# Feed-forward elementwise steps of a two-layer trunk: two-operand work on VectorE alone instead of VectorE and GpSimd

## The chip, the cores and the metric

The kernel runs on one core of one Trainium2 chip. The metric is device time in microseconds (us), the median of the runs. TensorE multiplies matrices, VectorE (DVE in the profile), ScalarE (ACT) and GpSimd (POOL) do elementwise work, SyncE (SP) issues the DMAs.

## The reference

A trunk of two layers over 1024 latent tokens and 256 context tokens, 1024 wide. Layer 0 has neighbourhood attention, layer 1 sliding-window attention; each layer then has a gated feed-forward network with a convolution over positions (width 2816, three taps). Everything is float32. What the change touches is the feed-forward network:

```python
def conv_ffn(h, w_up, conv_w, conv_b, w_down):
    t = h.shape[1]
    u = h @ w_up
    u_p = jnp.pad(u, ((0, 0), (CONV_W // 2, CONV_W // 2), (0, 0)))
    u = sum(u_p[:, tap:tap + t] * conv_w[tap] for tap in range(CONV_W)) + conv_b
    a, g = jnp.split(u, 2, axis=-1)
    return (a * jax.nn.silu(g)) @ w_down
...
        x = x + gt1 * (o @ w_out)
...
        h = modulate(rmsnorm(x, g_ffn[i]), sh2, sc2)
        x = x + gt2 * conv_ffn(h, ffn_w_up[i], ffn_conv_w[i], ffn_conv_b[i], ffn_w_down[i])
```

Layer 0 does the same for the context tokens.

## The kernel before, in words

**Precision.** Each operand of a matmul is split in two rounded parts, hi (a ScalarE copy) and lo (the operand less hi, a two-operand subtraction). A product is three matmuls: hi by hi, lo by hi, hi by lo. So each weight block that comes from memory (`wraw`, 128 x 1024) costs one ScalarE step (`whi`) and one subtraction (`wlo`).

**The up-projection.** It goes over 22 tiles of 128 channels (`plan_up`, lines 1680 to 1841), in a form with seven block products instead of eight (`PROD`, line 1675). Before the products, four two-operand steps on 128 x 512 (`s_op`, lines 1716 to 1725, tile `s`) make sums and differences of the two weight blocks; four `wlo` follow (three of 1024 columns, one of 512). TensorE writes the PSUM banks `ua`, `uc` and `ud`; a ScalarE copy or a VectorE add (`out_p`, line 1754) empties each into `c`, which frees the bank for TensorE. Then, for each half of the gate: ScalarE's centre tap makes `u` from `c`, two VectorE steps of three operands add the other taps (`u<-c,cv,u`, line 1797), SiLU goes over the gate half (ScalarE `u<-u`), and one product of 128 x 1024 multiplies the halves (`u<-u` as a two-operand step, line 1804). One or three subtractions (`ghit`, `glot`, lines 1824 to 1839) form the blocks for the down-projection, which go to `g_dram`. In layer 0, 40 small products for layer 1's modulation stand between these matmuls (line 1847).

**The down-projection** (`plan_pair`, line 1893) goes over 11 pairs of tiles in five passes; it loads `graw` from `g_dram` and `wraw`, splits both (`ghi`, `glo`, `whi`, `wlo`), forms weight differences in `s3`, and multiplies into `dn`. The results are added to `xn`.

**Around them** stand the output projection of the attention (`plan_oproj`; `oacc`, weights `woraw` split in `Oproj.weights`), the norms' sums of squares (`plan_sums`: ScalarE squares `sq`, two-operand adds into `nsum`), then `mp` and `bc`, two small groups of matmuls that average the sums and spread the result. In layer 0, `plan_next` prepares layer 1's norms, the rope tables `rc` and `rs` (always on GpSimd, line 2056) and the first weight slabs.

**What sets the order.** A planner, `Sched` (line 89), simulates the engines once while the program is built. Each step names its engine and a duration; a step with two engines goes to the one on which it would end first (`pick_engine`, line 156). A step takes its turn by a key among those that are ready; buffers come from rings (`caps`). The instructions are then written in the order found, and each engine runs its own in that order. The attentions of the two layers and the two feed-forward networks are four separate plans. Before the change most two-operand steps of the feed-forward plans name both engines:

```python
        LO = {512: (("dve", "pool"), (t_dve(512), t_pool(512))), 1024: (("dve", "pool"), (t_dve(1024), t_pool(1024)))}
        ADD = (("pool", "dve"), (t_pool(512), t_dve(512)))
...
            eng = LO[1024] if ft == FT - 1 else ("pool", t_pool(1024))
```

`LO` serves `wlo`, `glo` and the block differences, `ADD` the `s` steps and the last adds into `xn`; the product of the halves goes to GpSimd but for one tile of each layer. The planner counts 0.065 + n/960 us for VectorE and 0.15 + n/480 us for GpSimd.

Of the kernel before, what the change touches and what calls it, by code (L numbers as in the profile page):

```python
# [14 lines left out]
ALU = mybir.AluOpType  # L15
# [5 lines left out]
T = 1024  # L21
# [7 lines left out]
FT = FF // P  # L29
# [59 lines left out]
class Sched:  # L89
# [6 lines left out]
                                       pool=(0.15, 0.08, 0.06, 0.1), dma=(0.0, 0.0, 0.0, 0.0)).items()  # L96
# [145 lines left out]
def trunk_kernel(ctx, tc, xperm, xseq, cc, wmod, bmod, gnorm, na_wqkv, na_gq, na_gk, na_bias, na_wo,  # L242
# [3 lines left out]
    act, dve, pool, pe, dma = [InOrder(tc, e) for e in (nc.scalar, nc.vector, nc.gpsimd, nc.tensor, nc.sync)]  # L246
# [177 lines left out]
    ENG = dict(pe=pe, act=act, dve=dve, pool=pool, dma=dma)  # L424
# [4 lines left out]
    def t_dve(n):  # L429
        return 0.065 + n / 960.0  # L430
# [7 lines left out]
    def t_pool(n):  # L438
        return 0.15 + n / 480.0
# [374 lines left out]
    class Oproj:  # L814
# [3 lines left out]
        def __init__(self, sc, l, c, n, psa, gate, c_gate, w_gate):  # L818
            self.sc, self.l, self.c, self.n, self.psa, self.gate, self.c_gate, self.w_gate = sc, l, c, n, psa, gate, c_gate, w_gate
            self.ot, self.acc, self.w, self.raw = {}, {}, {}, {}  # L820

        def o_tiles(self, c):
            if c not in self.ot:
# [18 lines left out]
        def weights(self, i, src, key, uses, after=()):  # L842
            sc = self.sc

            def load(e):
                self.raw[i] = rpool.tile([P, 1024], F32, tag="raw", name="woraw")
                dma.dma_start(self.raw[i], src)

            def hi(e):
                self.w[i] = w_pair()  # L850
                act.activation(self.w[i][0], self.raw[i], AF.Copy)

            def lo(e):
                ENG[e].tensor_tensor(out=self.w[i][1], in0=self.raw[i], in1=self.w[i][0].bitcast(F32), op=ALU.subtract)
            r = ("woraw", i)
            sc.op("dma", 1.8, load, reads=self.w_gate + list(after), writes=[r], key=key, acq=[("raw", r, 2)])
            sc.op("act", t_act(1024), hi, reads=[r], writes=[("woh", i)], key=key, acq=[("w", ("wo", i), uses)], rel=[r])
            sc.op(("pool", "dve"), (2.28, 1.13), lo, reads=[r, ("woh", i)], writes=[("wol", i)], key=key, rel=[r])

        def project(self, dt, key, parts, evac):  # L860

# [17 lines left out]
    slabs = Slabs(na_wqkv, WL0)  # L879
# [100 lines left out]
    sc = Sched(dict(CAPS, klt=1))  # L980
# [282 lines left out]
    def ffn(l, opj, xt1, todo):  # L1263
# [8 lines left out]
        sc = Sched(dict(b=8, raw=3, w=WBUFS, x=8, sr=SRB, g=GB, g2=GB, sq=2), {"b", "raw", "w", "x", "sr", "g", "g2", "sq"})  # L1272
# [18 lines left out]
        def sub(e, out, a, b):  # L1291
            ENG[e].tensor_tensor(out=out, in0=a, in1=b, op=ALU.subtract)

        LO = {512: (("dve", "pool"), (t_dve(512), t_pool(512))), 1024: (("dve", "pool"), (t_dve(1024), t_pool(1024)))}
        ADD = (("pool", "dve"), (t_pool(512), t_dve(512)))

        X = [None] * 3
        n_todo = len(todo)
# [5 lines left out]
        def plan_sums(nm, n, x, xtok, key, rel=lambda k: (), make=None, ring="g", first=0):  # L1304

            J = {}
            I = (f"nm{nm}",)
            for k in [(first + k) % KT for k in range(KT)]:
                def sq(e, k=k):
                    if k == first:  # L1310
                        J["t"] = make(e) if make else sr_tile("nsum")
                        J[k] = J["t"]
                    elif ring == "g":
                        J[k] = gp.tile([P, 512], F32, tag="ghi", name="sq", bufs=GB)
                    else:
                        J[k] = D_["p"].tile([P, 512], F32, tag="sq", name="sq", bufs=2)
                    act.activation(J[k][:, :n], x(k), AF.Square)
                sc.op("act", t_act(n), sq, reads=[xtok(k)] + ([("dp",)] if ring == "sq" else []),
                      writes=[I + ("sq", k)] if k != first else [I + ("sums",)], key=key(k),
                      acq=[(ring, I + ("sq", k), 1)] if k != first else [("raw", I, 1) if make else ("sr", I, 9)], rel=rel(k))  # L1320
                if k != first:
                    def add(e, k=k):
                        ENG[e].tensor_tensor(out=J["t"][:, :n], in0=J["t"][:, :n], in1=J[k][:, :n], op=ALU.add)
                    sc.op(("pool", "dve"), (t_pool(n), t_dve(n)), add, reads=[I + ("sq", k), I + ("sums",)],
                          writes=[I + ("sums",)], key=key(k), rel=[I + ("sq", k)])
            return J

# [273 lines left out]
        def t34_(i):  # L1601
            if not t34:
# [3 lines left out]
              writes=[("dsh",)], key=-50)  # L1606
        rx = lambda c, k, n=1: [("xt", c, k // 2)] * n if c or not last else []
        kb = 46.0 * n_todo
        for k in range(KT):
            key = 46.0 * (1 if not last else 0) + k  # L1610
# [17 lines left out]
        for step in range(3):  # L1628
            for j in range(4):
                key = kb + (30.0 * j + 4 * step if not last else 2.0 * j + 8 * step)  # L1630
                sh = shift[:, j + 4:j + 5]
                if step == 0:
                    plan_t(1, 512, Nm[1], j, xap(1), xtok(1), scale, key)
                    sc.op("dve", t_dve(512), lambda e, j=j: dve.tensor_tensor(
                        out=X[0][:, j, :], in0=X[1][:, j, :], in1=X[0][:, j, :], op=ALU.subtract), reads=[("x", 1, j)],
                        writes=[("x", 0, j)], key=key)
                    parts(0, j, lambda j=j: t12h()[:, 2 * j, :], lambda j=j: t12l(j)[:, 0, :], ("t1", j), key, ())
                elif step == 1:
                    plan_t(1, 512, Nm[1], j + 4, xap(1), xtok(1), scale, key)
                    sc.op("dve", tst, stt(0, j, 1, j + 4, sh, 0, j), reads=[("x", 1, j + 4)], writes=[("x", 0, j)], key=key,  # L1640
                          rel=rx(1, j + 4))
                    parts(0, j, lambda j=j: t12h()[:, 2 * j + 1, :], lambda j=j: t12l(j)[:, 1, :], ("t2", j), key, rx(0, j))
                else:
                    sc.op("dve", tst, stt(1, j, 1, j + 4, dsh[:, j:j + 1], 1, j), reads=[("x", 1, j + 4), ("dsh",)],
                          writes=[("x", 1, j)], key=key, rel=rx(1, j + 4))
                    parts(1, j, lambda j=j: t34_(0)[:, j, :512], lambda j=j: t34_(1)[:, j, :512], ("t3", j), key, rx(1, j), hcs)
                    sc.op("dve", tst, stt(0, j + 4, 0, j + 4, sh, 0, j), reads=[("x", 0, j)], writes=[("x", 0, j + 4)], key=key,
                          rel=rx(0, j))
# [5 lines left out]
        for j in range(4):  # L1654
            key = kb + (30.0 * j + 12 if not last else 2.0 * j + 24)
            k = j + 4
            sc.op("act", t_act(512), lambda e, j=j, k=k: act.activation(b2h()[:, j, :], X[1][:, k, :], AF.Identity,
                                                                        bias=shift[:, k:k + 1]),
                  reads=[("x", 1, k), ("hcfree",)], writes=[("b2", j, "h")], key=key, rel=rx(1, k))
            sc.op("dve", tst, lambda e, j=j, k=k: dve.scalar_tensor_tensor(  # L1660
                out=b2l()[:, j, :], in0=X[1][:, k, :], scalar=shift[:, k:k + 1], in1=b2h()[:, j, :].bitcast(F32), op0=ALU.add,
# [18 lines left out]
        def plan_up(pos):  # L1680
            ft = FTS[pos]
            key = KU + 19.2 * pos
# [3 lines left out]
            T = lambda *a: ("up", ft) + a  # L1686
# [23 lines left out]
            def s_op(e, t, c, make, a, b, op):  # L1710
                if make:
# [5 lines left out]
                  reads=[rg],  # L1717
                  writes=[T("s", 1)], key=pk, acq=[("sr", T("s14"), 2)], rel=[rg])
# [4 lines left out]
                  reads=[ra, rg, T("s", 2)], writes=[T("s", 3)], key=pk, rel=[ra, rg])  # L1723
# [60 lines left out]
            for part in (1, 0):  # L1784
# [15 lines left out]
                    sc.op("dve", t_dve(1024) + 0.06, conv_, reads=cs, writes=[v], key=key - 10, rel=[ct])  # L1800
                if part:
                    sc.op("act", t_act(1024), lambda e: act.activation(V[1], V[1], AF.Silu), writes=[v], key=key - 10)
            eng = LO[1024] if ft == FT - 1 else ("pool", t_pool(1024))
            sc.op(*eng, lambda e: ENG[e].tensor_tensor(out=V[0], in0=V[0], in1=V[1], op=ALU.mult), reads=[T("v", 1)],
                  writes=[T("v", 0)], key=key - 10, rel=[T("v", 1)])


# [228 lines left out]
    def plan_next(sc, KS, xn, bank, x_tile, plan_sums, plan_bc, plan_t, plan_hilo, u_done):  # L2036
# [68 lines left out]
        for i in range(AHEAD):  # L2105
            key = KS[5] - 4
            sc.op("dma", 1.4, lambda e, i=i: slabs.load(i), reads=[("dw", 4, FT // 2 - 4, "r")], writes=[("slr", i)], key=key,
                  acq=[("raw", ("slr", i), 2)])
            sc.op("act", t_act(768), lambda e, i=i: slabs.hi(i), reads=[("slr", i), ("dw", 4, FT // 2 - 1, "wl", 0)],
                  writes=[("slh", i)], key=key, acq=[("w", ("slw", i), 1)], rel=[("slr", i)])  # L2110
            sc.op(("dve", "pool"), (0.87, 1.75), lambda e, i=i: slabs.lo(i, e), reads=[("slr", i), ("slh", i)],
                  writes=[("sll", i)], key=key, rel=[("slr", i)])

    slabs = Slabs(sw_wqkv, WL1)
# [356 lines left out]
```

## Time and profile before

| | us |
|---|---|
| median of 3 runs (2942.97 to 2950.92) | 2948.2 |
| the profiled execution | 2948.73 |
| its span, first to last instruction | 2947.0 |
| TensorE busy | 2829.2 |
| VectorE busy | 2406.0 |
| ScalarE busy | 1725.0 |
| GpSimd busy | 786.1 |

The span holds, in order: layer 0's attention to about 747 us, its output projection, the context's feed-forward network (860 to 1036), layer 0's up-projection (to 1498) and down-projection (to 1710), layer 1's attention (to 2190), its output projection and norms (to 2290), its up-projection (to 2726) and down-projection. An instruction's line is nearly always 79, that of the helper which records it, so steps are told apart by tile names: `out<-in`. "Idle before, releaser" says how long an engine stood still before a step and whose signal ended that. TensorE's busy time is modelled and its matmuls overlap; how often and for whom it waits tells more than its share.

### The profile page before, as it was taken

Reading aid. Unit: us, or ns where it says so; the run is one execution under the profiler, and the core shown is the slowest. Engines: PE = TensorE matmul, PEld = TensorE weight load, DVE = VectorE, ACT = ScalarE, POOL = GpSimd, SP = SyncE. Lnnn points to the kernel's source line nnn. Section 1 sums busy time; section 2 is a strip of 40 time slices with the busy share of each in tenths; the row PEclk is TensorE's granted clock in tenths of the full one; section 3 lists DMA queues with packets and bytes.
Section 4 is the critical chain, followed back from the end, with each engine's and each line's share of the span. In section 5 each row is a group of like instructions: output and inputs, shape, how many; then the busy total and the mean of one; then the engine's idle time right before and its main releaser. Section 6 shows DMA issues by size and latency. Waiting matters only on the chain. (4 is left out here: it accounts for less than half of the span.)

```text
span 2947.0 us, 46322 instructions
## 1 busy us (share of the span) xinstructions
PE 2829.2 (96%) x16344; PEld 2456.0 (83%) x16344; DVE 2406.0 (82%) x5112; ACT 1725.0 (59%) x3392; POOL 786.1 (27%) x860
## 2 busy tenths in 40 slices
PE   6999999999999999999989999999999999999999
PEld 4999999998789977777778888899877687777787
DVE  7888888889688788788786889999987887888757
ACT  4777777778456544444444558887863544444443
POOL 2222222223100034223340134544511123433200
PEclk9999999999999999999999999999999999999999
DMA  6222222214645544444465540000244332233655
GB/s 239 62 86 79 85 59 80 86 58 148 229 150 186 181 151 139 150 145 144 156 228 177 187 137 30 24 21 14 74 134 135 102 104 100 90 100 129 242 158 186
DMA packets 138842, 367.21 MB, mean 125 GB/s; under 512 B 20849, under 2 KB 30577, under 8 KB 137201
## 3 DMA queue, kind: packets, MB, share of 16 engines
q1 hardware_dynamic: 138608, 364.24, 37.3%
q8 instruction: 129, 2.11, 0.3%
q14 instruction: 105, 0.85, 0.1%
HBM read 297.21 MB, written 66.98 MB: 124 GB/s over the span
## 5 line engine op out<-in xcount | busy, mean ns | idle before, releaser
L79 DVE TENSOR_TENSOR wlo<-wraw,whi 128x512 fp32r<-128x512 f32 (+1 forms) x245 | 300.3, 1226 | 40.0 <-ACT whi L79 38.3
L79 ACT ACTIVATE whi<-wraw 128x512 fp32r<-128x512 f32 (+1 forms) x264 | 212.2, 804 | 164.5 <-PE ud L79 44.4
L79 ACT ACTIVATE whi<-s 128x1024 fp32r<-128x1024 f32 (+1 forms) x120 | 113.2, 944 | 256.0 <-PE uc L79 222.6
L79 DVE TENSOR_TENSOR ptlo<-pt,pthi 128x512 fp32r<-128x512 f32 (+2 forms) x384 | 223.1, 596 | 44.0 <-ACT pthi L79 41.8
L79 DVE SCALAR_TENSOR_TENSOR u<-c,cv,u 128x1023 f32<-128x1023 f32 x176 | 250.4, 1438 | 8.9 <-ACT u L79 7.3
L79 PE MATMUL dn<-glo,whi 128*128 128x512 f32 x616 | 242.7, 394 | 4.7 <-DVE glo L79 4.7
L79 PE MATMUL dn<-ghi,whi 128*128 128x512 f32 x616 | 242.7, 394 | 4.2 <-ACT ghi L79 4.2
L79 ACT ACTIVATE S<-S,m 128x640 f32<-128x640 f32 (+3 forms) x288 | 221.0, 768 | 43.2 <-DVE m L79 32.5
L79 PE MATMUL dn<-ghi,wlo 128*128 128x512 f32 x616 | 242.0, 393 | 0.0
L79 ACT ACTIVATE pthi<-pt 128x512 fp32r<-128x512 f32 (+2 forms) x384 | 194.3, 522 | 62.1 <-PE pt L79 53.0
L79 PE MATMUL pt<-idr,S 128*128 128x128 f32 x1280 | 198.3, 276 | 5.8 <-DVE S L79 2.7
L79 ACT ACTIVATE ghi<-graw 128x512 fp32r<-128x512 f32 x154 | 95.8, 629 | 170.8 <-PE dn L79 96.2
L79 PE MATMUL mm<-whi,h0hi 128*128 128x384 f32 x512 | 181.2, 354 | 1.6 <-ACT qraw L79 1.6
L79 POOL TENSOR_TENSOR u<-u 128x1024 f32<-128x1024 f32 x42 | 108.0, 2572 | 270.9 <-DMA wraw<-in_w_up_dram 104.4
L79 DVE TENSOR_TENSOR glo<-graw,ghi 128x512 fp32r<-128x512 f32 x145 | 104.2, 723 | 84.6 <-ACT ghi L79 84.0
L79 PE MATMUL mm<-wlo,h0hi 128*128 128x384 f32 x512 | 172.3, 336 | 0.0
L79 PEld LDWEIGHTS pt<-idr,S 128*128 128x128 f32 x1280 | 150.1, 141 | 19.1 <-DVE ptlo L79 3.5
L79 POOL TENSOR_TENSOR qy<-qv,mhalf 128x4 f32<-128x4 f32 (+2 forms) x120 | 125.0, 1043 | 140.7 <-DVE qv L79 131.7
L79 PE MATMUL pv<-ptlo,v 128*128 128x256 f32 (+1 forms) x688 | 154.0, 298 | 4.8 <-DVE ptlo L79 4.4
L79 PE MATMUL pv<-pthi,v 128*128 128x256 f32 (+1 forms) x688 | 149.6, 290 | 8.1 <-ACT pthi L79 3.7
L79 DVE TENSOR_TENSOR wlo<-s,whi 128x1024 fp32r<-128x1024 f32 (+1 forms) x114 | 133.8, 1174 | 28.7 <-ACT whi L79 27.7
L79 PE MATMUL ua<-t12hi,whi 128*128 128x512 f32 x352 | 141.5, 402 | 11.9 <-ACT c L79 8.2
(338 smaller groups left out, 9207.2 us busy)
## 6 DMA issues: line engine op xcount, KB each, us to landing
wraw<-in_w_up_dram SPq DMA_DIRECT2D x132, 512.0 KB, 3.4
wm<-in_wmod_dram SPq DMA_DIRECT2D x80, 512.0 KB, 4.2
wraw<-in_w_down_dram SPq DMA_DIRECT2D x44, 512.0 KB, 3.5
graw<-g_dram SPq DMA_DIRECT2D x44, 512.0 KB, 4.4
wraw<-in_w_down_dram SPq DMA_DIRECT2D x88, 256.0 KB, 3.1
graw<-g_dram SPq DMA_DIRECT2D x66, 256.0 KB, 2.8
slab<-in_na_wqkv_dram SPq DMA_DIRECT2D x32, 384.0 KB, 3.2
woraw<-in_na_wo_dram SPq DMA_DIRECT2D x24, 512.0 KB, 4.6
```

The costliest lines, as they stand in the source:

```text
L79: r = f(*a, **k)
```

## The change

Inside the feed-forward plans all two-operand elementwise steps name VectorE alone. `LO` and `ADD` become single-engine entries, with 0.03 us more per step in the planner's count; the product of the halves, the norms' adds, the output projection's weights inside these plans and the first slabs of layer 1 follow. GpSimd keeps its steps of the attention plans, the small power steps of the norms and the rope tables.

```diff
@@ Oproj
+            self.w_engs = ("pool", "dve"), (2.28, 1.13)
...
-            sc.op(("pool", "dve"), (2.28, 1.13), lo, reads=[r, ("woh", i)], writes=[("wol", i)], key=key, rel=[r])
+            sc.op(*self.w_engs, lo, reads=[r, ("woh", i)], writes=[("wol", i)], key=key, rel=[r])
@@ ffn
-        LO = {512: (("dve", "pool"), (t_dve(512), t_pool(512))), 1024: (("dve", "pool"), (t_dve(1024), t_pool(1024)))}
-        ADD = (("pool", "dve"), (t_pool(512), t_dve(512)))
+        LO = {n: ("dve", t_dve(n) + 0.03) for n in (512, 1024)}
+        ADD = LO[512]
+        opj.w_engs = LO[1024]
@@ plan_sums
-                    sc.op(("pool", "dve"), (t_pool(n), t_dve(n)), add, reads=[I + ("sq", k), I + ("sums",)],
+                    sc.op("dve", t_dve(n), add, reads=[I + ("sq", k), I + ("sums",)],
@@ plan_up
-            eng = LO[1024] if ft == FT - 1 else ("pool", t_pool(1024))
-            sc.op(*eng, lambda e: ENG[e].tensor_tensor(out=V[0], in0=V[0], in1=V[1], op=ALU.mult), reads=[T("v", 1)],
+            sc.op(*LO[1024], lambda e: ENG[e].tensor_tensor(out=V[0], in0=V[0], in1=V[1], op=ALU.mult), reads=[T("v", 1)],
@@ plan_next
-            sc.op(("dve", "pool"), (0.87, 1.75), lambda e, i=i: slabs.lo(i, e), reads=[("slr", i), ("slh", i)],
+            sc.op("dve", 0.87, lambda e, i=i: slabs.lo(i, e), reads=[("slr", i), ("slh", i)],
```

By the built programs 196 instructions leave GpSimd for VectorE: 42 products of 128 x 1024, 78 `s` steps, 23 `wlo` of 512 columns and 5 of 1024, 18 `ghit`, 9 `glo`, 9 `nsum`, and 12 others.

The planner finds new orders. First place: VectorE in layer 1's up-projection, one tile from the first `u` (taps of the gate half) to the add that empties `ud` (`c<-c,ud`). Before:

```order
L79 SCALAR_TENSOR_TENSOR u<-c_28507,cv,u 128x1023
L79 TENSOR_TENSOR wlo<-wraw,whi 128x512
L79 SCALAR_TENSOR_TENSOR u<-c_28507,cv,u 128x1023
L79 SCALAR_TENSOR_TENSOR u<-c_28468,cv,u 128x1023
L79 TENSOR_TENSOR s<-wraw,s 128x512
L79 SCALAR_TENSOR_TENSOR u<-c_28468,cv,u 128x1023
L79 TENSOR_TENSOR c_28612<-c_28612,ud 128x512
```

and now, in every second tile (the others keep the pattern above), with the four rows behind:

```order
L79 SCALAR_TENSOR_TENSOR u<-c_28779,cv,u 128x1023
L79 TENSOR_TENSOR s<-wraw 128x512
L79 SCALAR_TENSOR_TENSOR u<-c_28779,cv,u 128x1023
L79 TENSOR_TENSOR wlo<-s,whi 128x1024
L79 SCALAR_TENSOR_TENSOR u<-c_28745,cv,u 128x1023
L79 TENSOR_TENSOR s<-s,wraw 128x512
L79 TENSOR_TENSOR c_28885<-c_28885,ud 128x512
L79 SCALAR_TENSOR_TENSOR u<-c_28745,cv,u 128x1023
L79 TENSOR_TENSOR wlo<-wraw,whi 128x512
L79 TENSOR_TENSOR u<-u 128x1024
L79 TENSOR_TENSOR s<-wraw 128x512
```

Two `s` steps stand between the first `u` and the add, which now comes ahead of the last `u`; the product `u<-u` stands in VectorE's queue. TensorE's order in layer 1 is the same in both programs.

Second place: TensorE in layer 0's output projection, where the context's norm is averaged (`mp`).

```order
 L79 MATMUL oacc<-o0lo_10389,whi 128x512
 L79 MATMUL oacc<-o0hi_10385,wlo 128x512
-L79 MATMUL mp<-invd,nsum 128x1 x2
 L79 MATMUL oacc<-o0hi_10385,whi 128x512
 L79 MATMUL oacc<-o0lo_10389,whi 128x512
 L79 MATMUL oacc<-o0hi_10385,wlo 128x512
+L79 MATMUL mp<-invd,nsum 128x1 x2
```

`mp` moves three matmuls later; `bc`, some rows on, moves later as well.

## The prediction

> **What bounds the kernel now.** I read the page's busy times first (the first line below), then busy time by stage, then who TensorE waits for in the feed-forward stages, and last one stretch where it waits, instruction by instruction. The stages, in us from the span's start: 1036 to 1498 up-projection of layer 0, 1498 to 1710 its down-projection, 2190 to 2290 output projection and norms of layer 1, 2290 to 2726 its up-projection, 2726 to the end its down-projection. Columns: length, then busy time of PE, PEld, DVE, ACT and POOL, each with its count, and the granted clock:
>
> ```profile
> PE 2829.2 (96%) x16344; PEld 2456.0 (83%) x16344; DVE 2406.0 (82%) x5112; ACT 1725.0 (59%) x3392; POOL 786.1 (27%) x860
> ...
> 1036.00:1498.00 462.00, 458.60 (x2211) 355.43 (x2210) 369.32 (x366) 217.88 (x277) 151.44 (x75) 1.00 0.45 149
> 1498.00:1710.00 212.00, 203.96 (x891) 168.02 (x890) 169.06 (x244) 101.34 (x176) 43.36 (x29) 0.98 0.61 200
> 2190.00:2290.00 100.00, 92.01 (x420) 72.06 (x419) 70.36 (x103) 35.59 (x48) 12.37 (x7) 0.96 0.41 139
> 2290.00:2726.00 436.00, 418.79 (x1827) 337.83 (x1828) 365.38 (x337) 213.55 (x266) 142.98 (x70) 0.99 0.31 105
> 2726.00:2947.00 221.00, 213.47 (x927) 175.50 (x925) 150.94 (x215) 89.94 (x153) 25.50 (x16) 0.98 0.59 195
> ```
>
> TensorE sets the end nearly everywhere, so only its waits can be given back. What it waits for, first from 740 to 1730 us (layer 0), then from 2184 us to the end (layer 1); total us, times, longest:
>
> ```profile
> PE mp L79 <- DVE nsum L79: 5.7, 2, 3.7
> PE dn L79 <- DVE glo L79: 4.7, 1, 4.7
> PE uc L79 <- DVE wlo L79: 2.4, 1, 2.4
> PE bc L79 <- DVE nsum L79: 2.3, 1, 2.3
> PE dn L79 <- ACT ghi L79: 1.2, 1, 1.2
> ```
>
> ```profile
> PE ua L79 <- ACT c L79: 8.0, 7, 1.8
> PE ua L79 <- DVE c L79: 6.2, 8, 2.3
> PE ua L79 <- ACT t12hi L79: 3.5, 1, 3.5
> PE dn L79 <- ACT ghi L79: 3.0, 1, 3.0
> PE ua L79 <- DVE wlo L79: 2.5, 2, 2.0
> PE mp L79 <- DVE nsum L79: 2.0, 1, 2.0
> PE ua L79 <- DVE t12lo L79: 1.2, 2, 0.8
> PE ua L79 <- ACT whi L79: 0.9, 1, 0.9
> ```
>
> The first five come to 16.3 us, the next eight to 27.3 us: 43.6 us is what the edit could give back at most, but for stretches at a lower clock, which come after waits. Half of the second block is `ua` waiting for `c`: a PSUM bank of the up-projection that ScalarE or VectorE hasn't emptied yet.
>
> Why so late? One such wait ends at 2552.38. Start and length in us; VectorE, GpSimd, ScalarE, TensorE in turn:
>
> ```profile
> 2543.79 1.83 DVE L79 TENSOR_TENSOR wlo<-s,whi 128x1024 fp32r<-128x1024 f32 x1 [0.24 <-ACT whi L79]
> 2545.55 2.31 DVE L79 SCALAR_TENSOR_TENSOR u<-c,cv,u 128x1023 f32<-128x1023 f32 x1
> 2547.79 1.77 DVE L79 TENSOR_TENSOR wlo<-wraw,whi 128x512 fp32r<-128x512 f32 x1
> 2552.48 1.27 DVE L79 SCALAR_TENSOR_TENSOR u<-c,cv,u 128x1023 f32<-128x1023 f32 x1
> 2544.62 2.16 POOL L79 TENSOR_TENSOR s<-s,wraw 128x512 f32<-128x512 f32 x1
> 2546.86 2.15 POOL L79 TENSOR_TENSOR s<-wraw,s 128x512 f32<-128x512 f32 x1
> 2550.79 1.06 ACT L79 ACTIVATE u<-u 128x1024 f32<-128x1024 f32 x1 [3.03 <-DVE u L79]
> 2552.38 0.50 PE L79 MATMUL ua<-t12hi,whi 128*128 128x512 f32 x1 [1.39 <-ACT c L79]
> ```
>
> The convolution step `u` takes 2.31 us while GpSimd's `s` runs and 1.27 us a little later, when GpSimd is idle. ScalarE's SiLU waits 3.03 us for that `u`; the copy `c` stands behind it in ScalarE's queue, and TensorE waits 1.39 us for the copy. So GpSimd's steps reach TensorE by stretching VectorE's.
>
> **What VectorE gets back, and what it gets.** The stretched groups of layer 1's up-projection (2290 to 2726), and last two rows of the context stage (860 to 1030 us, GpSimd all but idle) for the clean price; count, busy us, mean ns:
>
> ```profile
> L79 DVE SCALAR_TENSOR_TENSOR u<-c,cv,u 128x1023 f32<-128x1023 f32 x84 | 113.9, 1374 | 0.7 <-ACT u L79 0.2
> L79 DVE TENSOR_TENSOR wlo<-wraw,whi 128x1024 fp32r<-128x1024 f32 x20 | 58.2, 2910 | 0.1
> L79 DVE TENSOR_TENSOR wlo<-s,whi 128x1024 fp32r<-128x1024 f32 x41 | 57.0, 1390 | 7.8 <-ACT whi L79 7.4
> L79 DVE TENSOR_TENSOR s<-wraw 128x512 f32<-128x512 f32 x34 | 32.1, 944 | 31.1 <-DMA wraw<-in_w_up_dram 31.1
> L79 DVE TENSOR_TENSOR wlo<-wraw,whi 128x512 fp32r<-128x512 f32 x24 | 22.9, 954 | 0.0
> L79 DVE TENSOR_TENSOR ghit<-u,glot 128x512 f32<-128x512 f32 x9 | 13.8, 1529 | 0.0
> L79 DVE TENSOR_TENSOR wlo<-wraw,whi 128x1024 fp32r<-128x1024 f32 x57 | 69.7, 1222 | 26.6 <-ACT whi L79 25.4
> L79 DVE TENSOR_TENSOR t12lo<-x,t12hi 128x512 fp32r<-128x512 f32 x7 | 4.8, 681 | 0.0
> ```
>
> Clean prices are thus 1.222 us for 1024 columns, 0.681 for 512, and 1.27 for `u`. Given back: `u` 84 x (1.374 - 1.27) = 8.7; `wlo` from `wraw` 20 x (2.910 - 1.222) = 33.8 (it meets GpSimd's 1024-column product nearly each time); `wlo` from `s` 41 x 0.168 = 6.9; `s` 34 x 0.263 = 8.9; `wlo` of 512 columns 24 x 0.273 = 6.6; `ghit` 9 x 0.848 = 7.6. Sum 72.5 us.
>
> What GpSimd does there:
>
> ```profile
> L79 POOL TENSOR_TENSOR u<-u 128x1024 f32<-128x1024 f32 x21 | 50.6, 2410 | 145.9 <-issue 61.3 <-DVE u L79 34.5 <-ACT whi L79 28.6
> L79 POOL TENSOR_TENSOR s<-s,wraw 128x512 f32<-128x512 f32 x15 | 31.8, 2118 | 50.7 <-DVE s L79 50.2
> L79 POOL TENSOR_TENSOR s<-wraw,s 128x512 f32<-128x512 f32 x17 | 29.2, 1720 | 20.1 <-DVE s L79 19.0
> L79 POOL TENSOR_TENSOR ghit<-u,ghit 128x512 f32<-128x512 f32 x7 | 15.1, 2151 | 0.5
> ```
>
> Moved to VectorE at the clean price: 21 x 1.222 = 25.7 and (15 + 17 + 7) x 0.681 = 26.6; with the ten left of this stage at 0.681 (nine more `s`, one `ghit`), 59.1 us. The net is 59.1 - 72.5 = -13 us on 365.4: VectorE ends with less busy time than now, about 352 of 436 us. Layer 0's up-projection is alike (70 to 75 steps of GpSimd in either stage), and in the kernel as a whole 196 instructions move.
>
> **What that is worth on TensorE, term by term**, against the profiled execution's own 2948.7 us (span 2947.0 and 1.7 around it; the median of the three runs is 2948.2, so the same number serves for both within 0.5).
>
> (a) Layer 1's up-projection. In the new order VectorE runs, from the first `u` of a tile to the second, u, s (or a `wlo` of 512 columns), u: 1.27 + 0.681 + 1.27 = 3.2 us. Now the two `u` of the quoted stretch start at 2545.55 and SiLU at 2550.79: 5.2 us. SiLU can start 2.0 us earlier, more than the 1.39 us wait behind it and more than the longest of the seven (1.8). So the 8.0 us go. The `wlo` and `whi` waits of this stage (2.0, the longer of the two `wlo` waits, and 0.9) go too. Of the `DVE c` waits I take half, 3.1 of 6.2: part of them comes from VectorE waiting in its queue for a weight (the 31.1 us behind `wraw` above), which the edit doesn't bring sooner. Sum 8.0 + 2.9 + 3.1 = 14.
>
> (b) Layer 0's up-projection: none. But for `bc`, counted in (d), no wait above is its own: the 40 modulation products that stand between its matmuls give VectorE more time per tile. Bounds 0 and 2 us.
>
> (c) Start of layer 0's down-projection, `dn` for `glo` 4.7 and for `ghi` 1.2. VectorE is ending the last up tiles there while the first `glo` come due, and GpSimd runs beside it (43.4 us in this stage, by its row). GpSimd keeps the rope tables, whose steps can still stretch VectorE's. I take 4 of 5.9.
>
> (d) The norms' sums, `mp` and `bc` behind `nsum`: 5.7 + 2.3 + 2.0 = 10.0. Steps of the sum leave GpSimd, with one hand-over less, and the order puts `mp` three matmuls later. The square on ScalarE still comes first. I take half: 5.
>
> (e) The rest: `t12hi`, `t12lo` and `ghi` of layer 1, 3.5 + 1.2 + 3.0 = 7.7, hang on ScalarE at least as much. I take 2.5. `uc` behind `wlo` (2.4): none.
>
> (f) The clock. In the rows above it stands at 0.98, 0.96, 0.99 and 0.98: 0.02 x 212 + 0.04 x 100 + 0.01 x 436 + 0.02 x 221 = 17 us of clock lost. As 25 of 44 us of waits go, some of it goes too; several of these stretches are changes of stage that stay. I take 3, bounds 0 and 8.
>
> Sum 14 + 0 + 4 + 5 + 2.5 + 3 = 28.5: 2948.7 - 28.5 = 2920.2, rounded 2921. Nothing is taken for the attentions: they are planned apart and keep their GpSimd steps.
>
> What hides the 59 us per stage: VectorE's own idle time, 436 - 365.4 = 71 us, and the 72.5 given back. If those are not given back, the cover is thin; that is the third rival.
>
> **Rivals.** *All waits go* (everything in the two blocks, 43.6 us, without the clock): 2948.7 - 43.6 = 2905. For it: every row but `t12hi` has a VectorE step as its releaser or right behind it. Against: `mp` hangs on ScalarE's squares too, and the first `dn` on a store of `g` and its load.
>
> *No change*: TensorE's waits for `c` come from the weights' arrival, not from the stretched steps, and the moved steps take up what is given back. For it: 31.1 us of VectorE's idle time is `wraw` from HBM, and 59.1 is close to 72.5. Against: the quoted stretch, where no DMA stands in the chain. Then only (c), (d) in part: 2948.7 - 5 = 2944.
>
> *Slower: VectorE's queue becomes the bound of the two up-projections.* It runs in order, and the moved steps stand ahead of the steps that empty banks. The price: 59.1 us on 22 tiles is 2.7 us a tile; what comes back is 72.5/22 = 3.3, a margin of 0.6. If the steps that come back are not on the way to `c` while the moved ones are, each tile of layer 1, which has no slack now, is late by up to 2.7 us (59 us in all), half of that if half of the moved steps stand behind `c`: 2948.7 + 30 = 2979. It decides when less than 2.7 of the 3.3 us comes back. Against: in the new order three `u`, one `wlo` of 1024 columns and two moved `s` stand from the first `u` to the add of `ud`, 3 x 1.27 + 1.222 + 2 x 0.681 = 6.4 us, where the trace of before has 8.2 (2545.55 to the end of the last `u`, 2552.48 + 1.27).
>
> A rule of the Trainium skill leans to this rival: "Perfetto Trace Analysis", "Identifying the Most-Contended Engine", takes the share of busy time of the Vector engine as a fair measure of how close it is to its limit. By it VectorE at 84% would go to (365.4 + 59.1)/436 = 97%, and adding to it would be wrong. The trace speaks against the measure here, since `wlo` of 1024 columns counts 2910 ns as busy beside 1222 ns for the same work.
>
> **How the numbers follow.** A measurement of this kernel can tell about 0.3%, 8.8 us. Forecast (2921, its own range 2908 to 2936): 0.70. All waits go: 0.12. No change: 0.10. Slower: 0.08. So faster by over 0.3% (under 2939) 0.82, within 0.10, slower 0.08. The range reaches from below the second case's 2905, with some clock, to the third case's 2944: 2902 to 2944. It leaves out the slower rival and a full return of the clock.
>
> **What would show it.** Right: in the profile after, `wlo` of 1024 columns at 1222 ns in both up-projections, `u` at 1.27 us; GpSimd busy about 410 us (786.1 less the 151.4 + 43.4 + 12.4 + 143.0 + 25.5 = 376 of the stages above); VectorE's busy time within 2% of 2406; `ua` behind `ACT c` under 2 us in all; layer 1's up-projection about 420 us instead of 436, layer 0's within 3 us of 462. Wrong: `wlo` still near 2.9 us (then GpSimd didn't stretch it); `ua` behind `DVE c` or `ACT c` longer than now at clean durations (queue order); an attention stage of another length (then something is moved that I hold fixed).

## The result

The changed kernel takes 2898.43 us (median of 6 runs, 2897.28 to 2903.0) against 2947.89 for the kernel before in the same comparison (6 runs, 2942.97 to 2950.92): ratio 0.9839, 95% interval 0.9829 to 0.985. That is 49.5 us less. The forecast of 2921 was about 27 us less than before, and its range ended at 2902. One execution of a later kernel (x11: 4562.01 us at a mean granted clock of 0.557, where the others show 0.98 to 0.99) is left out of every comparison below. The profiled execution took 2897.97 us, its span is 2896.2. Its busy times:

```profile
PE 2813.8 (97%) x16344; PEld 2452.9 (85%) x16344; DVE 2366.2 (82%) x5308; ACT 1725.5 (60%) x3392; POOL 406.5 (14%) x664
```

VectorE runs 196 more instructions and is busy 39.8 us less. TensorE's main waits, first in layer 0 (740 to 1710 us), then from 2184 us to the end:

```profile
PE mm L79 <- DVE cx L79: 2.5, 1, 2.5
PE uc L79 <- DVE wlo L79: 2.2, 1, 2.2
PE mp L79 <- DVE nsum L79: 2.0, 1, 2.0
PE mm L79 <- DVE wlo L79: 1.9, 1, 1.9
```

```profile
PE ua L79 <- ACT t12hi L79: 3.5, 1, 3.5
PE ua L79 <- DVE wlo L79: 1.4, 2, 0.9
PE ua L79 <- DVE t12lo L79: 1.2, 2, 0.8
PE ua L79 <- ACT whi L79: 0.9, 1, 0.9
```

Every wait of `ua` for `c` is gone, so are `dn` for `glo` and `ghi`, and `bc`. Of the two `mm` rows, the one behind `cx` stands at the end of layer 0's attention, outside the changed plans. The one behind `wlo` is a cost of the change. It is the start of layer 1's attention, which waits for one of the first weight slabs; the slab's `wlo` now stands in VectorE's queue behind eight adds into `xn` (5.35 us). Before, GpSimd ran it beside them, and the wait was 0.7 us.

Four of VectorE's groups in layer 1's up-projection (2252 to 2682):

```profile
L79 DVE SCALAR_TENSOR_TENSOR u<-c,cv,u 128x1023 f32<-128x1023 f32 x84 | 106.6, 1279 | 0.4
L79 DVE TENSOR_TENSOR wlo<-s,whi 128x1024 fp32r<-128x1024 f32 x42 | 51.4, 1223 | 12.0 <-ACT whi L79 12.0
L79 DVE TENSOR_TENSOR s<-wraw 128x512 f32<-128x512 f32 x43 | 29.3, 684 | 0.0
...
L79 DVE TENSOR_TENSOR wlo<-wraw,whi 128x1024 fp32r<-128x1024 f32 x20 | 24.4, 1218 | 0.2 <-ACT whi L79 0.2
```

The `wlo` from `wraw` takes 1218 ns instead of 2910, and `u` 1279 instead of 1374. The 31.1 us for which VectorE waited for `wraw` ahead of `s` read 0.0. The same place in a tile as the one that the prediction quoted, two rows from VectorE and two from ScalarE:

```profile
2510.25 1.28 DVE L79 SCALAR_TENSOR_TENSOR u<-c,cv,u 128x1023 f32<-128x1023 f32 x1
2512.05 1.28 DVE L79 SCALAR_TENSOR_TENSOR u<-c,cv,u 128x1023 f32<-128x1023 f32 x1
2513.47 1.04 ACT L79 ACTIVATE u<-u 128x1024 f32<-128x1024 f32 x1
2514.42 0.58 ACT L79 ACTIVATE c<-ua 128x512 f32<-128x512 f32 x1
```

From the first `u` to SiLU it is 3.2 us, as worked out, instead of 5.2. SiLU waits for nothing, and the copy `c` follows at once.

**Where the 50.8 us of span come from.** Both spans cut at each stage's first matmul: layer 0's output projection, the context's feed-forward network, layer 0's up- and down-projection, layer 1's output projection, up- and down-projection (layer 1's attention is left out). First before, then after; columns as in the prediction (length, PE, PEld, DVE, ACT, POOL, clock):

```profile
747.10:842.50 95.40, 91.75 (x410) 75.80 (x409) 63.97 (x94) 38.72 (x59) 10.44 (x7) 0.98 0.57 201
842.50:1036.10 193.60, 190.96 (x1577) 190.54 (x1576) 157.78 (x244) 115.77 (x172) 5.87 (x3) 0.99 0.52 175
1036.10:1498.50 462.40, 459.00 (x2213) 355.74 (x2212) 369.72 (x367) 218.28 (x277) 151.44 (x75) 1.00 0.45 149
1498.50:1721.60 223.10, 215.06 (x940) 177.22 (x939) 177.57 (x257) 105.92 (x183) 43.89 (x30) 0.98 0.61 200
...
2214.50:2260.80 46.30, 45.65 (x209) 37.72 (x208) 35.16 (x47) 18.92 (x25) 10.47 (x6) 1.00 0.37 125
2260.80:2726.30 465.50, 440.95 (x1931) 352.11 (x1930) 389.71 (x378) 223.78 (x281) 144.88 (x72) 0.98 0.31 105
2726.30:2947.00 220.70, 213.17 (x925) 175.26 (x923) 150.66 (x214) 89.64 (x153) 25.50 (x16) 0.98 0.59 196
```

```profile
746.70:842.00 95.30, 93.33 (x410) 77.08 (x409) 61.01 (x99) 37.97 (x57) 1.70 (x2) 0.96 0.57 201
842.00:1030.60 188.60, 186.38 (x1554) 186.16 (x1553) 152.52 (x242) 111.20 (x167) 1.01 (x1) 1.00 0.54 176
1030.60:1489.70 459.10, 459.10 (x2237) 357.62 (x2236) 359.64 (x445) 219.54 (x281) 1.08 (x1) 1.00 0.46 152
1489.70:1700.80 211.10, 211.10 (x941) 175.06 (x940) 173.49 (x277) 106.84 (x181) 7.75 (x7) 1.00 0.65 209
...
2196.00:2241.40 45.40, 45.40 (x209) 37.83 (x208) 35.70 (x55) 19.12 (x25) 1.01 (x1) 1.00 0.40 128
2241.40:2682.10 440.70, 433.50 (x1931) 351.17 (x1930) 368.58 (x447) 224.99 (x281) 1.01 (x1) 0.99 0.33 111
2682.10:2896.20 214.10, 209.62 (x925) 173.24 (x923) 150.70 (x231) 90.08 (x153) 0.00 (x0) 1.00 0.61 202
```

The lengths sum to 1707.0 before and 1654.3 after: 52.7 us less. (The 5.0 and 3.3 us of the second and third row belong together, since by the counts some 23 matmuls have moved from the one stage to the other.) Length less PE busy, TensorE's idle time, sums to 50.5 before and 15.9 after: 34.6 us less. The other 18.1 us are busy time for nearly the same matmuls, 8205 and 8207. They ran faster: by the clock column about 22 us were lost before (0.02 x 95.4 + 0.01 x 193.6 + 0.02 x 223.1 + 0.02 x 465.5 + 0.02 x 220.7) and 8 after (0.04 x 95.3 + 0.01 x 440.7), in a column rounded to 0.01. The trace's record of the granted clock, which that column averages, says it more exactly: TensorE has half clock for 44.5 us of these stages before and for 17.1 after, so 22.2 and 8.5 us were lost and 13.7 came back. Layer 1's attention took 492.6 us before and 495.0 after. Its plan is unchanged, and in the kernels below it took 491.8 to 499.5. By the same record it lost 6.8 us of clock before and 10.2 after; x11, which has the change too, took 492.7 there and lost 6.8.

### The profile page after: what moved, and what is told of

Its sections match the earlier page's. It is cut to its first block, busy times and chain, and to the rows that moved or that the text cites. A ratio compares the mean times of both kernels' runs of the same rounds, so it can differ in the third digit from the quotient of the medians.

```text
span 2896.2 us, 46130 instructions
## 1 busy us (share of the span) xinstructions
PE 2813.8 (97%) x16344; PEld 2452.9 (85%) x16344; DVE 2366.2 (82%) x5308; ACT 1725.5 (60%) x3392; POOL 406.5 (14%) x664
## 5 line engine op out<-in xcount | busy, mean ns | idle before, releaser
L79 DVE TENSOR_TENSOR wlo<-wraw,whi 128x512 fp32r<-128x512 f32 (+1 forms) x264 | 239.6, 908 | 44.7 <-ACT whi L79 43.9
L79 DVE TENSOR_TENSOR ptlo<-pt,pthi 128x512 fp32r<-128x512 f32 (+2 forms) x384 | 223.1, 596 | 44.2 <-ACT pthi L79 41.7
L79 DVE SCALAR_TENSOR_TENSOR u<-c,cv,u 128x1023 f32<-128x1023 f32 x176 | 223.3, 1279 | 5.8 <-ACT u L79 4.8
L79 POOL TENSOR_TENSOR n1y<-n1v,mhalf 128x4 f32<-128x4 f32 (+1 forms) x9 | 9.2, 1026 | 968.3 <-DVE n1v L79 967.2
```

The source lines that it names most:

```text
L79: r = f(*a, **k)
```

## The experiments

In the expectations S is the prediction's mechanism in its plain form: whatever stretches VectorE reaches TensorE. L is a rival: GpSimd's own results came late because the planner counts its steps too short. The other letters are explained where they stand. All ratios are against the kernel before.

**One part alone.** The kernel before with only the up-projection's steps on VectorE (x4), only the product of the halves (x5), and the whole change in layer 1's feed-forward plan only (x6):

```diff
 x4: in plan_up          sc.op(*LO[..]), sc.op(*ADD)       -> sc.op(*UP[..]),  UP[n] = ("dve", t_dve(n) + 0.03)
 x5: in plan_up          eng = ... else ("pool", t_pool(1024)) -> ... else ("dve", t_dve(1024) + 0.03)
 x6: in ffn, plan_next   the changed entries               -> only if l == 1, else those of before
```

> The kernel before, with only the up-projection's own steps moved to VectorE (sums s, wlo, product, block differences); norm sums, output-projection weights, context and down-projection steps keep both engines. Theory S, by the stage lengths before and after: layer 1's up-projection -24.8 us, layer 0's -3, part of the down-projections' -12 and -7: 2948 - 28 to 40 = 2908 to 2920 us. Theory L with the norm sums as the main late results: at most -15, 2933 us or more.

> The kernel before, with only the product of the halves (one step of 128 x 1024 per tile) on VectorE. Theory S: the product is what wlo of 1024 columns collides with, 33.8 of the 72.5 us of stretch in layer 1's up-projection; half or more of its 24.8 us go, little elsewhere: 2920 to 2937 us, and VectorE no longer waits for wraw (31.1 us before), because that weight was loaded late into a buffer that the stretched wlo held. If the wait for wraw comes from the weights' transfers themselves: it stays near 31 us and the time falls by less than 10: 2938 us or more.

> The change in layer 1's feed-forward network alone. By the stage lengths before and after (output projection and norms -1.0, up-projection -24.8, down-projection -6.6): 2948 - 32 = 2916 us, 2911 to 2921; layer 0 then holds the other 17 to 18 us. If the layers share their gain some other way (a faster layer 0 lets layer 1's weights come earlier), further than 8 us from 2916.

x4 took 2911.36 us, ratio 0.9886 (0.9872 to 0.9901); x5 2925.6, 0.9932 (0.9917 to 0.9947); x6 2915.92, 0.9902 (0.9887 to 0.9916). Layer 1's up-projection, 465.5 us before and 440.7 after, took 447.4 in x4, 450.2 in x5 and 441.5 in x6. Layer 1 thus brings about 30 of the 49 us. The product alone, of which 21 steps leave GpSimd in that stage, brings 15 of its 25 us, although GpSimd still does 100 us of other steps there. Two VectorE groups of x5 in that stage:

```profile
L79 DVE TENSOR_TENSOR wlo<-wraw,whi 128x1024 fp32r<-128x1024 f32 x21 | 27.7, 1317 | 0.1
...
L79 DVE TENSOR_TENSOR s<-wraw 128x512 f32<-128x512 f32 x25 | 17.1, 685 | 0.5 <-DMA wraw<-in_w_up_dram 0.3
```

With the product gone from GpSimd, `wlo` is back at 1317 ns and the wait for `wraw` falls from 31.1 us to 0.3. The edit touches no load. The trace of before shows how the two hang together (VectorE, GpSimd, SyncE's queue):

```profile
2554.27 3.09 DVE L79 TENSOR_TENSOR wlo<-wraw,whi 128x1024 fp32r<-128x1024 f32 x1
2561.56 0.69 DVE L79 TENSOR_TENSOR s<-wraw 128x512 f32<-128x512 f32 x1 [3.60 <-DMA wraw<-in_w_up_dram]
2553.88 2.40 POOL L79 TENSOR_TENSOR u<-u 128x1024 f32<-128x1024 f32 x1 [4.87 <-ACT whi L79]
2549.59 8.18 SPq L79 DMA_DIRECT2D wraw<-in_w_up_dram  x2
```

`wlo` is the last reader of its weight buffer. Beside the product it ends at 2557.36; SyncE's second load of the row ends its stay in the queue at 2557.77, and VectorE then waits 3.60 us for the data. Here the late weight follows from the stretched step.

**GpSimd work beside the changed kernel, which nobody waits for.** x1 adds 13 steps of 128x128 per tile that read and write a scratch tile, x2 the like as memsets, which only write:

```diff
+  pool.tensor_copy(scr[:, 0:1], t[:, 0:1])                                # starts beside the product or beside s
+  x1: pool.tensor_tensor(out=scr, in0=scr, in1=scr, op=ALU.add)           # 5 times, 4 and 4
+  x2: pool.memset(scr, 0.0)                                              # n // 50 times
```

> The kernel after, with GpSimd steps that nobody waits for put back into both up-projections: per tile 13 adds of 128 x 128 on a scratch tile, started by the arrival of the tile's data. They read the on-chip memory as the old steps did, but no result depends on them. Theory S (stretch: VectorE's steps with two operands in SBUF wait for GpSimd's reads): VectorE's wlo and u are longer again, it now carries the moved steps too, and both up-projections get longer: 2898 + 20 to 80 = 2920 to 2980 us. Theory L (late results: GpSimd's own steps were slow and the planner counted them too short): nothing waits for these, so 2895 to 2904 us.

> As the run with reading GpSimd steps, but the scratch steps are memsets, which only write; GpSimd is busy for a similar time in the same places. If the stretch comes from reads alone: VectorE's wlo stays at 1.22 us and the time at 2895 to 2906 us. If any work on GpSimd stretches VectorE: 2920 to 2980 us, as with reads. Theory L: 2895 to 2904 us.

x1 took 2898.08 us, ratio 0.9839 (0.9825 to 0.9854); x2 2897.85, 0.9836 (0.982 to 0.9853). Neither differs from the changed kernel, though GpSimd's added steps are busy 194.3 and 168.0 us in layer 1's up-projection. `wlo` there, in x1 and in x2:

```profile
L79 DVE TENSOR_TENSOR wlo<-wraw,whi 128x1024 fp32r<-128x1024 f32 x20 | 28.2, 1410 | 0.0
```

```profile
L79 DVE TENSOR_TENSOR wlo<-wraw,whi 128x1024 fp32r<-128x1024 f32 x20 | 24.4, 1219 | 0.6 <-ACT whi L79 0.6
```

Reads stretch VectorE, writes don't. But S, which gave x1 a loss, missed: these short reads stretch `wlo`, the large group that they hit hardest, by 0.2 us on average, and VectorE has the time. L's forecast for both came in, but L and a VectorE with time to spare say the same here. That left open whether long reads would do more.

**Long reads.** x10 gives the product alone back to GpSimd. x11 leaves it on VectorE and lets GpSimd square the spent half of `u` in place afterwards, once per tile; x12 does so three times; x13 fills the same buffer with zeros six times instead. In the traces of x12 and x13 TensorE, VectorE and ScalarE run the same instructions in the same order:

```diff
 x10: -  sc.op(*LO[1024], lambda e: ENG[e].tensor_tensor(out=V[0], in0=V[0], in1=V[1], op=ALU.mult), ...
      +  sc.op("pool", t_pool(1024), lambda e: ENG[e].tensor_tensor(out=V[0], in0=V[0], in1=V[1], op=ALU.mult), ...
 x11, x12: +  pool.tensor_tensor(out=V[1], in0=V[1], in1=V[1], op=ALU.mult)     # once; three times
 x13:      +  pool.memset(V[1], 0.0)                                            # six times
```

> The changed kernel with one part undone: the product of the halves (128x1024, once per tile) is GpSimd's again, 22 steps of about 2.4 us in each layer. Theory T (a long step of GpSimd that reads holds VectorE up for most of its length, and the late VectorE step holds the weight's buffer, so that the next load is issued late): the 1024-column lo of the first weight goes back from 1.22 us to about 2.8, VectorE waits for wraw again for 30 us or more, TensorE waits for c again, and layer 1's up-projection takes 450 to 455 us instead of 441; 2910 to 2920 us in all. Rival H (the few other steps of GpSimd, not this product, cost those 14 us where the product stayed and the planner's price was raised): the up-projection stays at 441, and the time is 2898 to 2902.

> The changed kernel with one more GpSimd step per tile that nobody's data come from: after VectorE's product, GpSimd squares the spent half of u in place (128x1024, about 2.4 us, reads and writes). It does nothing but read, write and keep that buffer 2 to 4 us longer. By theory T it stretches the VectorE steps beside it by 1 to 1.7 us per tile, 22 to 37 us of VectorE's busy time per layer, which VectorE's 72 us of idle time in layer 1's up-projection can take up: 2898 to 2908 us, less than where the product itself went back. By rival S (any stretch of VectorE reaches TensorE), 2910 to 2935. By rival N (what is stretched is only a step that works on the same tile as GpSimd's), no VectorE step gets longer and the time is 2898.

> The same with three such steps per tile, about 7.2 us of GpSimd in each tile of 20 us, about as much as it had before the change. By theory T VectorE loses 3.5 to 5 us per tile against 3.3 us of idle time in layer 1 and 4.5 in layer 0: VectorE becomes the bound, layer 1's up-projection takes 450 to 480 us instead of 441, and the whole 2910 to 2950 us. By rival N nothing is stretched: 2898 to 2902. If only the buffer that is kept longer costs anything, the groups of VectorE keep their 1.22 and 1.28 us and the time is over 2905.

> The control to the three long steps per tile: in their place GpSimd fills the same buffer with zeros six times (128x1024, about 1.1 us each, so about 6.7 us per tile), at the same places; the order on the other engines is the same. It writes and keeps the buffer as long, but reads nothing. By theory T (reads hold VectorE up, and what exceeds its idle time reaches TensorE) the groups of VectorE are back at 1.22 and 1.28 us, layer 1's up-projection at 441 us, and the time at 2896 to 2902 us, about 96 us less than with the reads. By the rival that the buffer kept longer costs those 96 us, it stays over 2950.

x10 took 2899.64 us, ratio 0.9844 (0.983 to 0.9858). x11: ratio 0.9847 (0.9828 to 0.9867), from three executions of 2894.44 to 2903.35 us. x12 took 2997.55, 1.0176 (1.0161 to 1.019), and x13 2900.41, 0.9841 (0.9825 to 0.9858). VectorE in layer 1's up-projection in x10:

```profile
L79 DVE TENSOR_TENSOR wlo<-wraw,whi 128x1024 fp32r<-128x1024 f32 x20 | 38.6, 1929 | 0.7
L79 DVE TENSOR_TENSOR s<-wraw 128x512 f32<-128x512 f32 x43 | 32.7, 760 | 5.2 <-DMA wraw<-in_w_up_dram 5.2
L79 DVE TENSOR_TENSOR s<-s,wraw 128x512 f32<-128x512 f32 x20 | 30.0, 1501 | 0.3
```

The steps are stretched again (1929 and 1501 ns instead of 1218 and 684), and yet the stage takes 441.7 us. So T (long reads stretch VectorE and make the weights late, 2910 to 2920 us) was wrong about the product's price: put back by itself, it costs nothing that can be measured. The time is the one that the rival H forecast, by which not the product but GpSimd's few other steps had cost time in x3 (below). VectorE is busy 382.71 us in the stage, 14 more than in the changed kernel though 22 products of 1.22 us are off it, and has the time for it. In x11 it has it for 31 us more (399.56 us busy). In x12 it no longer does. Layer 1's up-projection of x12 in a windows row, a row of TensorE's waits in that stretch, and a place from VectorE's and GpSimd's timelines; then the windows row of x13:

```profile
2278.80:2781.40 502.60, 454.59 (x1932) 360.17 (x1931) 466.75 (x447) 226.88 (x281) 149.68 (x64) 0.96 0.28 98
```

```profile
PE ua L79 <- DVE c L79: 38.8, 19, 2.7
```

```profile
2506.08 2.38 DVE L79 TENSOR_TENSOR s<-wraw,s 128x512 f32<-128x512 f32 x1
2508.39 2.38 DVE L79 TENSOR_TENSOR glot<-u 128x512 f32<-128x512 f32 x1
2510.69 2.91 DVE L79 TENSOR_TENSOR wlo<-s,whi 128x1024 fp32r<-128x1024 f32 x1
2513.52 0.67 DVE L79 TENSOR_TENSOR c<-c,ua 128x512 f32<-128x512 f32 x1
2505.70 6.81 POOL L79 TENSOR_TENSOR u<-u 128x1024 f32<-128x1024 f32 x3 [17.99 <-DVE u L79]
```

```profile
2246.50:2685.70 439.20, 431.97 (x1932) 350.22 (x1931) 368.33 (x446) 225.26 (x281) 121.56 (x127) 0.99 0.32 112
```

Three VectorE steps last 2.38, 2.38 and 2.91 us, one for each of GpSimd's three, and the add that empties `ua` starts behind them. VectorE is busy 98 us more than in the changed kernel, where 72 us were idle, and 36 us still are: the stretch of a tile comes in one piece, ahead of the add that TensorE waits for. The stage takes 62 us longer, 41 of them idle time of TensorE (502.60 - 454.59 = 48.0 instead of 7.2) and 21 busy time at a clock of 0.96. With writes at the same places (x13; 6.0 us of them in one such place, against the 6.8 us of reads shown) all of it is gone. So it is the reads that cost, and not the buffer kept longer, GpSimd being busy or the order. This is also the rule of the Trainium skill, "SBUF — State Buffer", "Who interferes with whom": a VectorE instruction with two inputs in SBUF contends with a GpSimd instruction that reads SBUF, not with one that only writes it. The trace agrees, with 1410 ns for `wlo` in x1 and 1219 in x2. The section also calls the shared ports an exclusive lock. In the two runs with reads, a VectorE step loses more beside longer GpSimd steps: 0.2 us on average beside the short ones of x1, 1.7 (2.91 less 1.22) beside one of 2.3 us in x12.

**The planner's price.** x3 is the kernel before, but its planner counts 0.8 + n/540 us for a GpSimd step instead of 0.15 + n/480, so that it gives GpSimd little but the product:

```diff
+        def t_pool(n):
+            return 0.8 + n / 540.0
```

> The kernel before, with the planner's price of a GpSimd step in the feed-forward plans raised to what the trace shows (0.8 + n/540 us: 1.75 for 512 columns, 2.70 for 1024); the product of the halves stays fixed on GpSimd, the other steps may still go to either engine. Theory L (the planner counted GpSimd too short): most of the gain, 2898 to 2912 us. Theory S: the product still stretches wlo and u, only part of the gain: 2922 to 2942 us.

It took 2922.3 us, ratio 0.9925 (0.991 to 0.9939), at the edge of what S forecast and 10 us or more above L's range. Layer 1's up-projection took 454.7 us. The same product on the same engine cost nothing in x10. Two VectorE groups of x3, then TensorE's main wait from 2340 us to the end of the stage:

```profile
L79 DVE TENSOR_TENSOR wlo<-wraw,whi 128x1024 fp32r<-128x1024 f32 x21 | 57.7, 2746 | 1.9
...
L79 DVE TENSOR_TENSOR s<-wraw 128x512 f32<-128x512 f32 x45 | 34.0, 755 | 52.7 <-DMA wraw<-in_w_up_dram 52.7
```

```profile
PE ua L79 <- DVE c L79: 5.2, 10, 1.7
```

Here the product meets `wlo`, the step that holds the weight buffer, in nearly every tile (2746 ns), and VectorE waits 52.7 us for the weights. In x10 it meets it in about half of them (1929 ns) and the `s` steps in the others, and the wait is 5.2 us. GpSimd's few other steps, H's explanation, all run before 2334 us in this stage of x3. From 2340 us on GpSimd runs the product alone, as in x10, and still TensorE waits 5.2 us for VectorE's `c` where in x10 it waits for nothing. So for these waits the place of the product counts, and with it the planner's order. What the late load costs by itself was not measured; a kernel with a third weight buffer would show it.

**What a wait of TensorE costs.** The changed kernel with a matmul per tile that adds zeros and waits for GpSimd, in layer 1's up-projection: x8 in each of the 22 tiles with two memsets ahead of it, x9 in every fourth with thirty.

```diff
+  pool.tensor_copy(scr[:, 0:1], C["1"][:, 0:1]); pool.tensor_tensor(out=scr[:, 0:1], in0=scr[:, 0:1], in1=scr[:, 0:1], op=ALU.subtract)
+  pool.memset(scr, 0.0)                                       # x8: 2, x9: 30 times
+  pe.matmul(U[d][:, 0:1], ones, scr[:, 0:1], start=False, ...)
```

> The kernel after, with a short forced wait of TensorE in each of the 22 tiles of layer 1's up-projection (a chain of few small GpSimd writes that ends in one 128 x 1 matmul adding zero): about 1 us each, 22 us in all. If a wait costs its length alone: 2898 + the sum of waits that the trace shows. If it also costs a restart of some 0.15 to 0.3 us: 3 to 7 us more than the sum. The granted clock should stay at 1.00 in this stage, since the waits are short.

> The same with 5 long forced waits instead of 22 short ones, about 4 to 6 us each, 20 to 30 us in all. If the clock is lost after long waits: the granted clock of this stage falls to about 0.97 or lower, and the time is the sum of waits plus 1.7 to 3.4 us per wait (8 to 17 us). If a wait costs its length alone: 2898 + the sum of waits, the clock at 1.00.

x8 took 2914.46 us, ratio 0.9898 (0.9882 to 0.9915), but not as meant: only four of its 22 waits came about (8.6 us in all, the longest 3.7); GpSimd was done in time for the others, whose added matmuls (a pair in the trace) cost 0.24 us. The stage takes 459.2 us, 18.5 more than in the changed kernel, where the waits and 22 such pairs come to 13.9. The clock of the stage, expected at 1.00, stands at 0.98 (0.99 in the changed kernel): two of the waits were longer than meant. x9 took 2946.95, 1.0003 (0.9993 to 1.0012), the time of the kernel before: its five waits sum to 36.0 us and the stage takes 488.1 us, 47.4 more than in the changed kernel. One of the five, on TensorE:

```profile
2340.16 0.59 PE L79 MATMUL ua<-scr,ones 128*128 128x1 f32 x2 [8.46 <-POOL scr L79]
...
2343.32 0.63 PE L79 MATMUL ua<-t12hi,whi 128*128 128x512 f32 x1
2343.74 0.49 PE L79 MATMUL ua<-t12lo,whi 128*128 128x512 f32 x1
...
2344.31 0.39 PE L79 MATMUL ua<-t12hi,whi 128*128 128x512 f32 x1
```

Up to 2343.7 the matmuls start 0.43 us apart instead of 0.23. So these waits cost 47.4 / 36.0 = 1.3 times their length, 1.25 without the five pairs of added matmuls (0.45 us each). Told per wait, that is (47.4 - 36.0 - 5 x 0.45) / 5 = 1.8 us on top of its length, which weighs more on a shorter wait.

None of these kernels beats the changed one: x1, x2, x10, x11 and x13 are level with it, the others slower.

One thing these runs leave open. They show that stretched steps cost time in one and the same order (x12 against x13), but none keeps the order of before with its steps at their clean durations. So how much of the 24.8 us of layer 1's up-projection is the stretch and how much the planner's new order is not separated.

## Why the forecast was too small

The direction, the mechanism and the clean durations were right: `wlo` 1218 and `u` 1279 ns, GpSimd busy 406.5 us (about 410 forecast), VectorE 2366.2 (within 2% of 2406). In layer 1's up-projection VectorE's busy time fell by 21 us (389.71 to 368.58) where 13 were worked out. The sizes on TensorE were not right. 52.7 us came back in the feed-forward stages where the terms gave 28.5, and layer 1's attention, held fixed, took 2.4 longer. The step that failed most is (f), the clock: 3 us were taken and 18.1 us of busy time came back. Next is the half of the `DVE c` waits in (a) that was left standing. (A slip besides: 2920.2 rounds to 2920.)

(a) Layer 1's up-projection, 14 forecast. What failed here is the half left of the `DVE c` waits, for "a weight (the 31.1 us behind `wraw` above), which the edit doesn't bring sooner". It does: in the stretch shown above the load goes out when the stretched `wlo` lets go of the buffer, and with the product moved (x5) the wait falls from 31.1 us to 0.3. All 14.2 us of waits for `c` went. Of the 2.9 us for `wlo` and `whi`, only about 1 went (2.5 to 1.4; 0.9 stays). TensorE's idle time in the stage fell by 17.4 us, and its busy time by 7.5 more, which belongs to (f).

(b) Layer 0's up-projection, 0 (bounds 0 to 2). Together with the context's network ahead of it, it got 8.3 us shorter: 3.8 of idle time, of which `bc` (2.3) was counted in (d), and 4.5 of busy time. A wait of `dnc` for `glo` (0.8), which the rows quoted didn't reach, and the clock of both stages (1.7 us lost in each before, none after) had been left out.

(c) Start of layer 0's down-projection, 4 of 5.9: all 5.9 went, and the stage has no idle time left (8.04 to 0, with an `mp` of 2.1 that (d) had). With its clock back at 1.00 that is 12.0 us.

(d) The norms' sums, 5 of 10: 8.0 went; one `mp` of 2.0 stays, in layer 0.

(e) The rest, 2.5 of 7.7: `ghi` 3.0 went, `t12hi` 3.5 and `t12lo` 1.2 stay.

(f) The clock, 3 (bounds 0 to 8): 18.1 us of busy time came back, 13.7 of them by the clock record; what the other 4 are is open. This is the largest miss. I had counted a wait at its own length and taken most of the lost clock for changes of stage that stay. x9 shows a wait taking about 1.8 us more than its length, with matmuls 0.43 us apart behind it. Layer 1's down-projection is the plainest case: its one wait of 3.0 us went and the stage is 6.6 us shorter.

So of the miss, 9 us are waits (34.6 of idle time against 25.5 in (a) to (e)) and 15 busy time, most of it the clock.

The rivals: *all waits go* came nearest, with 2905, but by errors that offset each other: only 32.4 of its 43.6 us of waits went by the rows, and the clock, which it left out, carried the time past it. *No change* falls with the result, and its reason with x5, where the weight wait goes with the product. *VectorE's queue as the bound* did not happen, with 368.58 us busy in 440.70, 84%, where the prediction had worked out 97% by the occupancy rule of the Trainium skill ("Perfetto Trace Analysis", "Identifying the Most-Contended Engine"). x12, at 93%, shows that such a loss can happen.

What the prediction didn't see is that the parts don't add. In layer 1's up-projection the product alone (x5) gives 15.3 us and all the rest without it (x10) 23.8, of 24.8 in all. Behind the rest the product is worth another 1.0 us, while behind the product the rest still brings 9.5.

## What to carry to other kernels

When one engine's steps stretch another's, set the stretch of a tile against the idle time that the stretched engine has ahead of the step for which the bounding engine waits. Here a stretch below that was free (x10, x11), one above it was paid in waits (x12), and the parts of the change didn't add. Before calling a wait for a load independent, look at which step frees the load's buffer and whether that step is one of the stretched ones. Count a removed wait of TensorE of some microseconds at more than its length, since the slow restart behind it can go too.

## What the runs showed of the hardware

The waits that x8 was to have were expected to be too short to cost any clock, but a wait of 2.4 us can be followed by half clock. In the kernel before, `uc` waits 2.39 us for `wlo` until 867.73 and `ua` 2.34 us for `c` until 2483.38; the two windows rows behind these waits:

```profile
868.20:871.60 3.40, 3.40 (x19) 3.40 (x18) 3.40 (x7) 1.01 (x3) 0.00 (x0) 0.50 0.61 196
...
2484.00:2488.00 4.00, 4.00 (x19) 3.29 (x18) 4.00 (x5) 2.93 (x4) 1.56 (x1) 1.00 0.00 0
```

One is at 0.50 of the clock, the other at 1.00. The Trainium skill, "TensorE: Matmul & The Clock Gate", "What's actually happening", has the clock fall after an idle window of about 3.4 us, counted by windows that run on by themselves. The trace agrees with a fall that depends on when the wait comes, but 2.39 us have been enough. In this trace's record of the granted clock every stretch at half clock begins a whole number of steps of 3.413 us after another, one of them at 868.2. On that grid TensorE is idle for 2.4 us of the interval that ends at 868.2, while the point 2482.7 cuts the second wait into 1.7 and 0.7 us. That fits, but it is argued from two waits: no run moved a wait along the grid, and elsewhere in this trace intervals with 1.1 and 1.5 us idle lost the clock and one with 1.8 kept it.
